# Turning the SwiGLU product f by 32x32 blocks on VectorE and a round trip through DRAM

## The chip, the cores and the metric

One core of a Trainium2 chip runs the whole kernel. The metric is device time in microseconds (us), and the median of several runs is compared. In the profile PE is TensorE (PEld its weight loads), DVE is VectorE, ACT is ScalarE, POOL is GpSimd and SP is SyncE, whose queue issues nearly all transfers.

## What is computed

A stack of transformer blocks on 256 tokens of width 1024, in fp32: four SwiGLU FFNs with a gMLP mixer and an MLA attention mixer between them, then a second block (retention and forgetting attention side by side) with a fifth FFN. The change touches the FFNs only:

```python
def swiglu(n, w_gate, w_up, w_down):
    return (jax.nn.silu(n @ w_gate) * (n @ w_up)) @ w_down

f = swiglu(rms_norm(h, ffn_pre_g[layer, 0]), ffn_w_gate[layer, 0], ffn_w_up[layer, 0], ffn_w_down[layer, 0])
h = h + 0.5 * rms_norm(f, ffn_post_g[layer, 0])
```

The inner width is 2816, so there are 11 groups of 256 inner columns.

## The kernel before

The 256 tokens are two tiles of 128 (called tile 0 and tile 1; `t` in the code). All weights stream once through the chip as chunks of 128 x 1024 values (512 KB) that both tiles use: tile 0 takes chunk s at step s, tile 1 five steps later (LAG). For each chunk SP loads `raw` (3 buffers, line 158), ACT rounds it to `hi` (line 337) and DVE computes the rest `lo` = raw - hi (line 338), both in rings of 9 buffers. Every fp32 product is then three fast matmuls, hi by hi, lo by hi and hi by lo (lines 167 to 169).

An FFN walks over the 11 groups. For group j, `up(j)` takes four chunks and gives `g`, 128 tokens by 256 gate and 256 up columns, in PSUM. ACT applies Tanh (`th`, line 364), DVE forms (th + 1) * gate (line 365) and f (line 367): 128 tokens by 256 inner columns. The product with w_down needs f with the inner columns on the partitions. `turn(j)` does that two steps later: two 128x128 transposes on PE into PSUM (`tr`, line 376), from where ACT and DVE make the pair `fth`, `ftl` (lines 337 and 338 again). `down(j-1)` takes two chunks of w_down and adds to the accumulators `a`, after `up(j)`. So in the middle of an FFN the work repeats with a period of one group for both tiles: six chunks, 72 matmuls, two Tanhs, six hi, six lo and two turns. Below this is called a round.

`later(st, n, fn)` puts a function off by n steps of its tile. The program is written in that order, but a scheduler at build time places each engine's instructions by priority, so the order on each engine comes from it. Each engine runs its own list strictly in order.

The two lines that decide when f is turned and used are

```python
later(st, 2, turn, j)
if 0 < j < NG - 2 * last:
    yield from down(j - 1)
```

Of the kernel before, what the change touches and what calls it, by code (L numbers as in the profile page):

```python
# [9 lines left out]
F32 = mybir.dt.float32  # L10
F32R = mybir.dt.float32r
# [5 lines left out]
P = 128  # L17
D = 1024
KD = D // P
FF = 2816  # L20
NG = FF // 256
# [88 lines left out]
def body(ctx: ExitStack, tc: tile.TileContext, a: dict, out: bass.AP, stop=None, dbg=None):  # L110
    nc = tc.nc
    V, S, G, PE = nc.vector, nc.scalar, nc.gpsimd, nc.tensor

    base = ctx.enter_context(tc.tile_pool(name="base", bufs=1))
    ring = ctx.enter_context(tc.tile_pool(name="ring", bufs=1))
    psg = ctx.enter_context(tc.tile_pool(name="psg", bufs=2, space=bass.MemoryType.PSUM))
    psa = ctx.enter_context(tc.tile_pool(name="psa", bufs=1, space=bass.MemoryType.PSUM))
    pst = ctx.enter_context(tc.tile_pool(name="pst", bufs=2, space=bass.MemoryType.PSUM))

    def f32(x):  # L120
        return x.bitcast(F32)
# [70 lines left out]
    def later(st, n, fn, *args):  # L192

        st.later.append([n + 1, fn, args])
# [128 lines left out]
    def acc_tile(st):  # L323
        return [psa.tile([P, 512], F32, name=f"a{st.t}{q}") for q in range(2)]

    def g_tile():
        return psg.tile([P, 512], F32, name="g")
# [8 lines left out]
    def split(hi, lo, src):  # L336
        S.copy(hi, src)  # L337
        V.tensor_tensor(lo, src, f32(hi), op=ALU.subtract)  # L338

    def rows_gemm(acc, lhs, w, k, first, last):  # L340

        for q in range(2):
            mm3(acc[q], sl(lhs, slice(None), k), sl(w, slice(None), slice(512 * q, 512 * q + 512)), first, last)

    def unit(st, ps, lhs=None, nq=4, nk=2, n=512):

        for q in range(nq):
            w = yield
            k_gemm(ps, lhs or st.xt, w, nk * q, q == 0, q == nq - 1, nk, n)
# [7 lines left out]
    def ffn(st, inner={}, last=False):  # L357
        fts = {}

        def up(j):  # L360
            ps = g_tile()
            yield from unit(st, ps)
            th = base.tile([P, 256], F32, name="th", tag="th", bufs=2)
            S.activation(th, ps[:, :256], AF.Tanh, scale=st.ch)  # L364
            V.scalar_tensor_tensor(th, th, 1.0, ps[:, :256], op0=ALU.add, op1=ALU.mult)  # L365
            f = base.tile([P, 256], F32, name="f", tag="f", bufs=2)
            V.scalar_tensor_tensor(f, th, st.cc, ps[:, 256:], op0=ALU.mult, op1=ALU.mult)  # L367
            fts[j] = f
            st.mark = f[:, 0:1]
            later(st, 2, turn, j)  # L370

        def turn(j):
            f = fts[j]
            tr = pst.tile([P, 4, P], F32, name="tr")
            for k in range(2):
                PE.transpose(tr[:, k, :], f[:, k * P:(k + 1) * P], ident)  # L376
            pool, n = (enter("last"), 6) if last and j > 5 else (base, 3)
            hi = pool.tile([P, 2, P], F32R, name="fth", tag="fth", bufs=n)
            lo = pool.tile([P, 2, P], F32R, name="ftl", tag="ftl", bufs=n)
            split(hi, lo, tr[:, :2, :])  # L380
            fts[j] = hi, lo

        def down(j):
            if j == 0:
                st.acc = acc_tile(st)
            for k in range(2):
                w = yield
                f = fts[j]
                rows_gemm(st.acc, f, w, k, j + k == 0, j == NG - 1 and k == 1)

        for j in range(NG):
            yield from up(j)
            if 0 < j < NG - 2 * last:
                yield from down(j - 1)
            if callable(inner.get(j)):
                inner[j]()
            elif j in inner:
                yield from inner[j]
        for j in range(NG - 1 - 2 * last, NG):
            yield from down(j)  # L400
# [614 lines left out]
    def enter(name):  # L1015
        if name not in pools:
            pools[name] = [tc.alloc_tile_pool(name=name, bufs=1), 0]
        return pools[name][0]
# [92 lines left out]
    n = len(chunks)  # L1111
# [38 lines left out]
def layout(i):  # L1150

    c = np.ascontiguousarray
    o = {}

    def cols(w, unit, nk=2):

        k, n = w.shape
        return c(w.reshape(k // (P * nk), nk, P, n // unit, unit).transpose(3, 0, 2, 1, 4)).reshape(-1, P, nk * unit)

    def rowsw(w):  # L1160

        return w.reshape(-1, P, w.shape[1])

    def gu(g, u):
        both = np.stack([g.reshape(D, NG, 256), u.reshape(D, NG, 256)], 2).reshape(D, NG * 512)
        return cols(both, 512)

    fl = [(i["ffn_w_gate"][l, k], i["ffn_w_up"][l, k], i["ffn_w_down"][l, k]) for l in range(2) for k in range(2)]
    fl.append((i["w_gate_2"][0], i["w_up_2"][0], i["w_down_2"][0]))
    for n, (g, u, d) in enumerate(fl):  # L1170
        o[f"gu{n}"] = gu(g, u)
        o[f"dn{n}"] = rowsw(d)
    o["win"] = cols(i["gmlp_w_in"][0], 512)
    o["wgo"] = rowsw(i["gmlp_w_out"][0])
    o["wdq"] = cols(i["mla_w_dq"][0], 512)
    o["wdkv"] = cols(i["w_dkv"], 320)
    uq = i["mla_w_uq"][0].reshape(512, NH, 192)
    o["wuqr"] = cols(c(uq[:, :, P:]).reshape(512, 512), 512)
    o["wuq"] = cols(c(uq[:, [0, 2, 4, 6, 1, 3, 5, 7], :P]).reshape(512, 1024), 512)
    ukv = i["w_ukv"].reshape(256, NH, 256)  # L1180
    o["wukv"] = np.concatenate([cols(c(ukv[:, :, k * P:(k + 1) * P]).reshape(256, 1024), 512) for k in range(2)])
    wo = i["mla_w_o"][0].reshape(NH, P, D)
    o["wo"] = c(wo[[0, 2, 4, 6, 1, 3, 5, 7]])
    w2 = i["w_in_2"][0]
    big = np.concatenate([w2[:, 1536:2048], w2[:, 2048:2560], w2[:, 2560:3072], w2[:, 0:512], w2[:, 512:1024],
                          w2[:, 1024:1536], w2[:, 3080:4104], w2[:, 4104:5128]], 1)
    o["w2"] = cols(big, 512)
    o["w2f"] = c(w2[:, 3072:3080].reshape(8, P, 8).transpose(1, 0, 2)).reshape(P, 64)
    o["wro"] = rowsw(i["w_ret_o_2"][0])
    o["wfo"] = rowsw(i["w_fox_o_2"][0])  # L1190
    o["wout"] = rowsw(i["w_out_2"][0])
    gl = [i["ffn_pre_g"][0, 0], i["ffn_pre_g"][0, 1], i["ffn_pre_g"][1, 0], i["ffn_pre_g"][1, 1], i["mix_pre_g"][0],
          i["mix_pre_g"][1], i["kv_norm_g"], i["kv_a_norm_g"], i["mla_q_norm_g"][0], i["g_mix_2"][0], i["g_ffn_2"][0], i["g_ret_norm_2"][0],
          np.concatenate([i["g_fox_q_2"][0]] * 2), np.concatenate([i["g_fox_k_2"][0]] * 2)]
    o["pre"] = np.stack([gl[k] for k in (4, 1, 2, 5, 3, 9)])
    o["kva"], o["qn"] = i["kv_a_norm_g"].reshape(1, 256), i["mla_q_norm_g"].reshape(1, 512)
    o["gains"] = c(np.concatenate([g.reshape(-1, P).T for g in gl], 1))
    o["ffn_post_g"] = c(i["ffn_post_g"].reshape(4, D))
    o["mix_post_g"] = c(i["mix_post_g"])
    o["gmlp_ln_g"] = c(i["gmlp_ln_g"])  # L1200
    o["gmlp_ln_b"] = c(i["gmlp_ln_b"])
    o["b_forget_2"] = c(i["b_forget_2"])
    o["ws"] = c(i["gmlp_w_s"][0].transpose(2, 0, 1)).reshape(P, 16 * P)
    o["bs"] = c(i["gmlp_b_s"][0].T)
    o["x"] = c(i["x"][0])
    o["positions"] = c(i["positions"].reshape(2, P).T)
    o["c1"], o["c2"] = constants()
    return o
# [49 lines left out]
```

## Time and profile before

| | us |
|---|---|
| median of three runs | 1397.67 (1396.39 to 1398.02) |
| the profiled execution | 1396.79 |
| its span (first to last instruction) | 1394.9 |
| PE busy | 1376.0, 99% |
| DVE busy | 957.0, 69% |
| ACT busy | 717.2, 51% |
| DMA, mean | 182 GB/s |

Busy time is the union of an engine's instructions; issuing a transfer or waiting is not counted as busy. Matmuls overlap in the rows, so the step from one start to the next tells what a matmul costs. A row's idle time is what passed on that engine just before the instruction, with what ended it.

### The profile page before, as it was taken

The page shows a single profiled execution, that of the slowest core. Times are in us where ns is not written, and L with a number is a line of the kernel's source. Part 1 is how long each engine was busy: PE and PEld are TensorE (multiplying, and loading weights), DVE is VectorE, ACT ScalarE, POOL GpSimd, SP SyncE. Part 2 cuts the span into 40 slices and gives each one's busy share as a digit, 9 for nine tenths or more (in the row PEclk, how much of TensorE's full clock was granted, in tenths as well). Part 3 has the DMA queues.
Part 4 walks back from the last instruction along what each step waited for, and adds up shares of the span by engine and source line. Part 5 has one row for each costly group of instructions (what it writes and reads, how often), then busy time and mean ns, then how long its engine had stood idle before and what let it go on. Part 6 is the DMA issues. An engine that isn't in the chain of part 4 may idle for free.

```text
span 1394.9 us, 17750 instructions
## 1 busy us (share of the span) xinstructions
PE 1376.0 (99%) x6402; PEld 1125.1 (81%) x6402; DVE 957.0 (69%) x1530; ACT 717.2 (51%) x1043; POOL 59.7 (4%) x81
## 2 busy tenths in 40 slices
PE   8999999999999999999999999999999999999998
PEld 5888887887788887888877888888878788888887
DVE  7775579977757558775569676665677865765554
ACT  6644456555544445544456655444567544544442
POOL 0000020000000001000001010000020000000000
PEclk9999999999999999999999999999999999999999
DMA  7666667554566664666655336666544355565662
GB/s 250 201 220 185 188 250 222 157 191 151 181 191 217 186 192 143 201 220 195 188 190 179 124 130 183 202 201 191 199 137 150 119 168 183 171 190 185 192 185 88
DMA packets 71656, 254.45 MB, mean 182 GB/s; under 512 B 8592, under 2 KB 10000, under 8 KB 71184
## 3 DMA queue, kind: packets, MB, share of 16 engines
q1 hardware_dynamic: 70992, 252.78, 57.7%
q8 instruction: 51, 0.84, 0.2%
q10 hardware_dynamic: 576, 0.52, 0.1%
q14 instruction: 37, 0.30, 0.1%
HBM read 252.23 MB, written 1.05 MB: 182 GB/s over the span
## 4 chain that ended last, share of the span: by engine, by line
PE 87%; DVE 6%; ACT 2%; DMA 2%; issue 1%; POOL 1%; SPq 0%; DVEq 0%; ACTq 0%; POOLq 0%
PE g L167 16%; PE g L168 16%; PE g L169 16%; PE a L169 11%; PE a L167 11%; PE a L168 11%; DVE lo L338 2%; PE tr L376 2%; PE tr L217 2%; DMA raw<-in_win 1%; POOL sm L145 1%; ACT hi L337 1%; DMA raw<-in_gu 1%; PE tr L459 0%; PE tr L722 0%
## 5 line engine op out<-in xcount | busy, mean ns | idle before, releaser
L338 DVE TENSOR_TENSOR lo<-raw,hi 128x1024 fp32r<-128x1024 f32 (+2 forms) x462 | 560.8, 1216 | 307.2 <-ACT hi L337 305.6
L337 ACT CAST hi<-raw 128x1024 fp32r<-128x1024 f32 (+2 forms) x462 | 481.2, 1044 | 428.8 <-PE g L169 205.7
L167 PE MATMUL g<-hi,xth 128*128 128x512 f32 x1040 | 414.3, 398 | 2.2 <-ACT hi L337 1.8
L168 PE MATMUL g<-lo,xth 128*128 128x512 f32 x1040 | 407.6, 392 | 2.0 <-DVE lo L338 2.0
L169 PE MATMUL g<-hi,xtl 128*128 128x512 f32 x1040 | 406.3, 391 | 0.0
L167 PEld LDWEIGHTS g<-hi,xth 128*128 128x128 f32 x1040 | 195.4, 188 | 43.0 <-ACT hi L337 3.5
L169 PEld LDWEIGHTS g<-hi,xtl 128*128 128x128 f32 x1040 | 195.4, 188 | 41.3 <-DVE sm L255 0.2
L168 PEld LDWEIGHTS g<-lo,xth 128*128 128x128 f32 x1040 | 195.6, 188 | 41.0 <-DVE lo L338 3.7
L167 PE MATMUL a<-hi,fth 128*128 128x512 f32 x440 | 175.7, 400 | 0.0
L168 PE MATMUL a<-lo,fth 128*128 128x512 f32 x440 | 172.0, 391 | 0.0
L169 PE MATMUL a<-hi,ftl 128*128 128x512 f32 x440 | 171.9, 391 | 0.0
L169 PEld LDWEIGHTS a<-hi,ftl 128*128 128x128 f32 x440 | 82.6, 188 | 17.4
L364 ACT ACTIVATE th<-g,ch 128x256 f32<-128x256 f32 x110 | 52.3, 475 | 86.4 <-PE g L169 85.2
L168 PEld LDWEIGHTS a<-lo,fth 128*128 128x128 f32 x440 | 82.8, 188 | 15.5
L167 PEld LDWEIGHTS a<-hi,fth 128*128 128x128 f32 x440 | 82.6, 188 | 15.5
L167 PE MATMUL a<-hi,xth 128*128 128x512 f32 x232 | 94.0, 406 | 0.7 <-ACT xth L337 0.6
L168 PE MATMUL a<-lo,xth 128*128 128x512 f32 x232 | 91.0, 394 | 0.0
L169 PE MATMUL a<-hi,xtl 128*128 128x512 f32 x232 | 90.9, 395 | 0.0
L365 DVE SCALAR_TENSOR_TENSOR th<-th,g 128x256 f32<-128x256 f32 x110 | 45.9, 418 | 43.5 <-ACT th L364 43.4
L337 ACT CAST fth<-tr 128x256 fp32r<-128x256 f32 x110 | 40.5, 369 | 37.6 <-PE tr L376 37.6
L367 DVE SCALAR_TENSOR_TENSOR f<-th,cc,g 128x256 f32<-128x256 f32 x110 | 52.8, 480 | 3.5
L167 PEld LDWEIGHTS a<-hi,xth 128*128 128x128 f32 x232 | 43.6, 188 | 10.3 <-ACT xth L337 2.1
(318 smaller groups left out, 1187.0 us busy)
## 6 DMA issues: line engine op xcount, KB each, us to landing
raw<-in_gu SPq DMA_DIRECT2D x220, 512.0 KB, 3.6
raw<-in_dn SPq DMA_DIRECT2D x110, 512.0 KB, 3.9
raw<-in_w SPq DMA_DIRECT2D x40, 512.0 KB, 3.3
raw<-in_win SPq DMA_DIRECT2D x32, 512.0 KB, 4.3
raw<-in_wgo SPq DMA_DIRECT2D x16, 512.0 KB, 3.6
raw<-in_wo SPq DMA_DIRECT2D x8, 512.0 KB, 3.3
raw<-in_wout SPq DMA_DIRECT2D x8, 512.0 KB, 3.3
gn<-in_pre SPq DMA_DIRECT2D x6, 512.0 KB, 5.3
```

The lines of the kernel that those rows point to most:

```text
L145: G.tensor_tensor(o, i, hp if up else hn[:, :n], op=ALU.pow)
L167: PE.matmul(o, l[0], r[0], start=start, stop=False)
L168: PE.matmul(o, l[0], r[1], start=False, stop=False)
L169: PE.matmul(o, l[1], r[0], start=False, stop=stop_)
L217: PE.transpose(tr[:, k, :], src[:, (4 * ngroup + k) * P:(4 * ngroup + k + 1) * P], ident)
L337: S.copy(hi, src)
L338: V.tensor_tensor(lo, src, f32(hi), op=ALU.subtract)
L364: S.activation(th, ps[:, :256], AF.Tanh, scale=st.ch)
L365: V.scalar_tensor_tensor(th, th, 1.0, ps[:, :256], op0=ALU.add, op1=ALU.mult)
L367: V.scalar_tensor_tensor(f, th, st.cc, ps[:, 256:], op0=ALU.mult, op1=ALU.mult)
L376: PE.transpose(tr[:, k, :], f[:, k * P:(k + 1) * P], ident)
```

## The change

For 10 of the 11 groups PE no longer turns f. DVE turns it in place by 32x32 blocks (`V.transpose`, into `ft`), which leaves the blocks themselves where they were: partition block a holds columns i of its own 32 tokens. `away` writes `ft` to a DRAM tile `far` (128 pieces of 1 KB), and `back` reads it again with four transfers, one for each block c of 32 columns, so that the blocks a of the tokens come to lie side by side on the 32 partitions (32 x 4 pieces of 256 bytes each). `parts` makes `fth` and `ftl` from the SBUF tile `fr`. All five transfers are issued from ACT's queue. The last group of each FFN keeps `turn`. `ft` shares its buffers with `th`, `fr` with `f`. The columns come out in another order within a group, so the rows of w_down are laid out in that order on the host, before the launch.

```diff
+    dram = ctx.enter_context(tc.tile_pool(name="dram", bufs=1, space=bass.MemoryType.DRAM))
@@ up(j)
             st.mark = f[:, 0:1]
-            later(st, 2, turn, j)
+            if j == NG - 1:
+                later(st, 2, turn, j)
+                return
+
+            ft = base.tile([P, 256], F32, name="ft", tag="th", bufs=2)
+            V.transpose(ft, f)
+            later(st, 1, away, j, ft)
+
+        def away(j, ft):
+            far = dram.tile([4, 32, 4, 64], F32, name="far", bufs=4)
+            nc.scalar.dma_start(far.rearrange("a i c r -> (a i) (c r)"), ft)
+            later(st, 0, back, j, far)
+
+        def back(j, far):
+            fr = base.tile([P, 4, 64], F32, name="fr", tag="f", bufs=2)
+            for c in range(4):
+                nc.scalar.dma_start(fr[32 * c:32 * c + 32], far[:, :, c, :].rearrange("a i r -> i a r"))
+            later(st, 0, parts, j, fr.rearrange("p a (k i) -> p k a i", k=2))
+
+        def parts(j, fr):
+            f = fts[j] = f_tiles(j)
+            split(*(x.rearrange("p k (a i) -> p k a i", a=4) for x in f), fr)
@@ layout
-        o[f"dn{n}"] = rowsw(d)
+        d = d.reshape(NG, 4, 2, 32, D)
+        o[f"dn{n}"] = np.concatenate([d[:-1].transpose(0, 2, 1, 3, 4).reshape(-1, P, D), d[-1].reshape(2, P, D)])
```

`f_tiles(j)` only names the pool and makes the two result tiles, as `turn` did before.

ACT's list in one round in the middle of the first FFN, before (`th_1327` is tile 1's Tanh, `th_1344` tile 0's; `hi` are weight chunks; numbers name single buffers):

```order
L337 CAST hi_1293<-raw_1291 128x1024
L337 CAST hi_1311<-raw_1309 128x1024
L337 CAST hi_1334<-raw_1332 128x1024
L364 ACTIVATE th_1327<-g_1239,ch_290 128x256
L337 CAST hi_1357<-raw_1355 128x1024
L364 ACTIVATE th_1344<-g_1259,ch_168 128x256
L337 CAST hi_1383<-raw_1381 128x1024
L337 CAST hi_1409<-raw_1407 128x1024
L337 CAST fth_1377<-tr_1374 128x256
L337 CAST fth_1397<-tr_1394 128x256
```

The same round after the change, from tile 0's Tanh to the end of its turn (lines are those of the changed file, one higher here; `far_1305` and `fr_1328` belong to tile 1, `far_1319` and `fr_1346` to tile 0):

```order
L365 ACTIVATE th_1292<-g_1199,ch_170 128x256
L381 DMA far_1305<-ft_1278 128x256
L338 CAST hi_1335<-raw_1333 128x1024
L338 CAST hi_1363<-raw_1361 128x1024
L387 DMA fr_1328<-far_1305 32x4x64
L381 DMA far_1319<-ft_1297 128x256
L387 DMA fr_1328<-far_1305 32x4x64 x3
L387 DMA fr_1346<-far_1319 32x4x64 x4
L338 CAST fth_1357<-fr_1328 128x256
L338 CAST hi_1385<-raw_1383 128x1024
L338 CAST hi_1403<-raw_1401 128x1024
L338 CAST fth_1373<-fr_1346 128x256
```

Before, the two casts of the turned f stood behind each other and read PSUM; now ten transfers stand in the list, and the first read of tile 0 stands three issues behind the write it reads from.

PE's list at the end of tile 1's part of a round, before (`tr` are the turns, `a00` and `a01` tile 0's accumulators):

```order
L376 MATMUL tr_1374<-cst_70,f_1330 128x128 x2
L167 MATMUL a00_331<-hi_1334,fth_1263 128x512
L168 MATMUL a00_331<-lo_1335,fth_1263 128x512
L169 MATMUL a00_331<-hi_1334,ftl_1264 128x512
L167 MATMUL a01_332<-hi_1334,fth_1263 128x512
L168 MATMUL a01_332<-lo_1335,fth_1263 128x512
L169 MATMUL a01_332<-hi_1334,ftl_1264 128x512
L376 MATMUL tr_1394<-cst_70,f_1347 128x128 x2
L167 MATMUL g_1373<-hi_1223,xth1_225 128x512
```

And after, from the end of tile 1's `up` on (`g_1181` is tile 1's, `g_1199` tile 0's, `a10` and `a11` are tile 1's accumulators):

```order
L170 MATMUL g_1181<-hi_1093,xtl1_230 128x512
L168 MATMUL a10_477<-hi_1111,fth_1211 128x512
L169 MATMUL a10_477<-lo_1112,fth_1211 128x512
L170 MATMUL a10_477<-hi_1111,ftl_1212 128x512
L168 MATMUL a11_478<-hi_1111,fth_1211 128x512
L169 MATMUL a11_478<-lo_1112,fth_1211 128x512
L168 MATMUL g_1199<-hi_1239,xth0_130 128x512
L170 MATMUL a11_478<-hi_1111,ftl_1212 128x512
L168 MATMUL a10_477<-hi_1136,fth_1211 128x512
L169 MATMUL a10_477<-lo_1137,fth_1211 128x512
L170 MATMUL a10_477<-hi_1136,ftl_1212 128x512
```

The turns are gone from the list, and the two tiles' matmuls now lie in another order: tile 0's last `up` chunk stands between the parts of tile 1's `down`.

## Rows read from the trace of the kernel before

**Rows 1.** The page: span, busy time of each engine, and the chain's shares by engine.
```profile
span 1394.9 us, 17750 instructions
...
PE 1376.0 (99%) x6402; PEld 1125.1 (81%) x6402; DVE 957.0 (69%) x1530; ACT 717.2 (51%) x1043; POOL 59.7 (4%) x81
...
PE 87%; DVE 6%; ACT 2%; DMA 2%; issue 1%; POOL 1%; SPq 0%; DVEq 0%; ACTq 0%; POOLq 0%
...
```

**Rows 2.** The chain that ended last, in shares by engine and line.
```profile
...
by line: PE g L167 16.1%; PE g L168 16.0%; PE g L169 16.0%; PE a L169 10.8%; PE a L167 10.8%; PE a L168 10.7%; DVE lo L338 1.8%; PE tr L376 1.7%; PE tr L217 1.7%; issue 1.5%; DMA raw<-in_win 1.0%; POOL sm L145 1.0%; ACT hi L337 1.0%; DMA ra
...
```

**Rows 3.** Busy time by stretch; this one is mid first FFN, columns in its head.
```profile
...
core 0: us, PE busy (x) PEld busy (x) DVE busy (x) ACT busy (x) POOL busy (x), PEclk, DMA share, GB/s
26.00:178.00 152.00, 152.00 (x687) 124.93 (x686) 98.62 (x162) 76.76 (x104) 2.04 (x3) 1.00 0.65 201
...
```

**Rows 4.** Timeline of PE: start and length in us; 27 matmuls from the first row to the second.
```profile
...
109.62 0.39 PE L167 MATMUL g<-hi,xth 128*128 128x512 f32 x1
...
115.51 0.40 PE L169 MATMUL a<-hi,ftl 128*128 128x512 f32 x1
115.75 0.38 PE L376 MATMUL tr<-cst,f 128*128 128x128 f32 x2
115.88 0.48 PE L167 MATMUL a<-hi,fth 128*128 128x512 f32 x1
116.20 0.40 PE L168 MATMUL a<-lo,fth 128*128 128x512 f32 x1
...
```

**Rows 5.** Timeline of ACT, same stretch; in brackets the idle time before and what ended it.
```profile
...
110.50 0.47 ACT L364 ACTIVATE th<-g,ch 128x256 f32<-128x256 f32 x1 [1.67 <-PE g L169]
110.87 1.04 ACT L337 CAST hi<-raw 128x1024 fp32r<-128x1024 f32 x1
111.86 0.48 ACT L364 ACTIVATE th<-g,ch 128x256 f32<-128x256 f32 x1
113.26 1.05 ACT L337 CAST hi<-raw 128x1024 fp32r<-128x1024 f32 x1 [0.93 <-PE a L169]
...
127.36 0.47 ACT L364 ACTIVATE th<-g,ch 128x256 f32<-128x256 f32 x1 [1.67 <-PE g L169]
...
```

**Rows 6.** Groups by line and shape: count, busy us, mean ns, idle us before.
```profile
...
L338 DVE TENSOR_TENSOR lo<-raw,hi 128x1024 fp32r<-128x1024 f32 x454 | 554.9, 1224 | 303.0 <-ACT hi L337 301.4
L337 ACT CAST hi<-raw 128x1024 fp32r<-128x1024 f32 x454 | 476.0, 1050 | 424.6 <-PE g L169 204.7 <-PE a L169 155.3 <-DMA raw<-in_gu 28.8
...
L367 DVE SCALAR_TENSOR_TENSOR f<-th,cc,g 128x256 f32<-128x256 f32 x110 | 52.8, 480 | 3.5
L364 ACT ACTIVATE th<-g,ch 128x256 f32<-128x256 f32 x110 | 52.3, 475 | 86.4 <-PE g L169 85.2 <-DVE cc L259 1.1
L365 DVE SCALAR_TENSOR_TENSOR th<-th,g 128x256 f32<-128x256 f32 x110 | 45.9, 418 | 43.5 <-ACT th L364 43.4
...
L338 DVE TENSOR_TENSOR ftl<-tr,fth 128x256 fp32r<-128x256 f32 x110 | 42.4, 417 | 5.9 <-ACT fth L337 5.8
...
L337 ACT CAST fth<-tr 128x256 fp32r<-128x256 f32 x110 | 40.5, 369 | 37.6 <-PE tr L376 37.6
...
L337 ACT CAST xth<-y 128x256 fp32r<-128x256 f32 x16 | 6.3, 402 | 7.0 <-DVE y L228 6.8
...
```

**Rows 7.** DMA queues, and issues by tile: count, KB each, median us to landing.
```profile
...
q1 hardware_dynamic: 70992, 252.78, 57.7%
...
q10 hardware_dynamic: 576, 0.52, 0.1%
...
out<-h SPq DMA_DIRECT2D x4, 128.0 KB, 1.9
out<-h ACTq DMA_DIRECT2D x4, 128.0 KB, 2.9
...
gain<-in_gains SPq DMA_DIRECT2D x1, 42.0 KB, 2.8
wfr<-in_w2f SPq DMA_DIRECT2D x1, 32.0 KB, 3.9
...
```

**Rows 8.** Line 1098, the stores of the result: issue in ns, and us to landing.
```profile
...
L1098 ACTq DMA_DIRECT2D out<-h x4: 338/338/374, 1383.5 to 1392.0; - x4
...
DMA to landing us min/median/max: 1.7/1.9/4.0
```

**Rows 9.** Line 158, the weight loads: us to landing.
```profile
...
DMA to landing us min/median/max: 3.0/3.6/9.8
```

**Rows 10.** The same line in the first FFN alone, 26 to 178 us.
```profile
...
DMA to landing us min/median/max: 3.3/4.1/6.7
```

More of the change, by code (lines that the diff above doesn't have):

```diff
@@ L369, in up, with f_tiles @@
             st.mark = f[:, 0:1]
-            later(st, 2, turn, j)
+            if j == NG - 1:
[13 more added lines that the diff above has]
+            later(st, 0, parts, j, fr.rearrange("p a (k i) -> p k a i", k=2))
+        def f_tiles(j):
+            pool, n = (enter("last"), 6) if last and j > 5 else (base, 3)
+            return tuple(pool.tile([P, 2, P], F32R, name=x, tag=x, bufs=n) for x in ("fth", "ftl"))
+        def parts(j, fr):
+            f = fts[j] = f_tiles(j)
+            split(*(x.rearrange("p k (a i) -> p k a i", a=4) for x in f), fr)
         def turn(j):
@@ L376, in turn @@
                 PE.transpose(tr[:, k, :], f[:, k * P:(k + 1) * P], ident)
[L377 to L381, printed above, removed]
+            fts[j] = f_tiles(j)
+            split(*fts[j], tr[:, :2, :])
         def down(j):
```

## The prediction, made before the changed kernel was run

> **What bounds the kernel now.** I read the page first. TensorE (PE) is busy for 1376.0 of 1394.9 us, ScalarE (ACT) for 51% and VectorE (DVE) for 69% [rows 1]; the chain that ended last lies on PE for 87% and on DVE, ACT and DMA together for 10% [rows 1]. A busy PE says little by itself, since matmuls overlap, so I went to stretches: in the first FFN PE has work in every one of 152 us, at the full granted clock of 2.4 GHz [rows 3]. In the timeline of PE 26 steps from the matmul at 109.62 to that at 115.51 take 5.89 us, so one 128x512 matmul costs 0.2265 us of PE, whatever its row calls its length [rows 4]. A pair of turns (the two 128x128 transposes of f) stands in that rhythm as a hole: from 115.51 to 116.20 there are 0.69 us where two steps would take 0.453, so the pair costs 0.236 us [rows 4]. Now ACT: between the Tanh of one round of groups and that of the next lie 16.86 us (110.50 to 127.36) [rows 5]. A round is one group of both token tiles, that is six chunks, 72 matmuls and two pairs: 72 x 0.2265 = 16.31, and 0.55 is left for two pairs. ACT waits for PE there, not the reverse: of 424.6 us of idle time before the hi casts, 360.0 end with a matmul [rows 6]. So PE sets the pace of the FFNs, and what leaves its queue there leaves the span, as long as nobody else becomes the slower one.
>
> **What the change removes.** 100 pairs of turns (10 groups, 2 tiles, 5 FFNs). At 0.236 us that is 23.6 us. From below: the chain gives the turns' line 1.7% of 1394.9 us, 23.7 us for 110 pairs, 0.216 each, so 21.6 for 100 [rows 2]. From above: the 0.55 us of a round, 0.27 a pair, 27 [rows 5]. I take 23.6, since it was read at the pair itself.
>
> **What it adds on DVE.** One 32x32 block turn of 128x256 for each group and tile. No such row exists; other 128x256 operations take 0.418 and 0.480 us, and one on four times the elements 1.224 [rows 6], so 0.42 to 1.22, and I take 0.48, that of the f product which reads and writes the same tile shape. 100 x 0.48 is 48 us on an engine that is idle for 31% [rows 1]: nothing on the path. Its one reader is the write: tile 0's turn stands behind a lo and is done some 7.0 us after tile 1's Tanh (3.4 for the 15 matmuls between the two Tanhs, then 0.47, 0.34, 1.05, 1.22 and 0.48), and the round worked out below wants it at 7.7; at 1.22 us it would come just then. The cast and the difference that make fth and ftl stay in number, but read SBUF instead of PSUM; a cast of the same size from SBUF takes 0.402 against 0.369 [rows 6], 3 us on ACT in all, hidden.
>
> **What it adds on ACT and the DMA queues.** Five issues for each group and tile, 500 in all; one on ACT's queue takes 0.338 us [rows 8], 169 us on an engine with 678 us free. The packets: 128 written and 512 read, and 16 completions for each of five, 720 a turn, 72,000 in all. ACT's queue now has 576 packets for 0.1% [rows 7]; by that these cost 12.5% (6 to 19% with the rounding), and the engines' share goes from 57.7% to about 70%. They don't fill up, but loads, writes and reads will land somewhat later than today.
>
> **The new waits.** In the order of the changed kernel ACT does, in a round: Tanh of tile 1, two hi, Tanh of tile 0, write of tile 1, two hi, first read of tile 1, write of tile 0, three more reads, four reads of tile 0, fth of tile 1, two hi, fth of tile 0. ACT works in order, so the first read of tile 0 holds it until the write three issues earlier has landed, and fth holds it until the reads have. Behind these waits stand the two hi casts, then the next Tanh and two more hi; PE waits for the hi, and DVE's lo and SyncE's next weight load follow each hi. What can set the pace is therefore this round on ACT, DVE and SP: Tanh 0.47, hi 1.05, its lo 1.22, the weight load whose buffer this lo freed, hi 1.05, one read's issue 0.34, the write's landing, 1.01 for three more issues, the reads' landing, fth 0.37. The fixed parts are 5.51 us [rows 6, 8]; three landings come on top, and the whole must stay under PE's 16.31, so the three may sum to 10.8 us. The loads land after 3.6 us in the median of the kernel, 3.0 at best [rows 9], and after 4.1 in the first FFN [rows 10]; I take 3.9. For the write: stores of 128 KB land after 1.7 to 4.0, with 1.9 the median, 2.9 from ACT's queue [rows 7, 8]; I take 2.6, near the median of all, and above it, because loads are in flight here. For reads in 256-byte pieces the nearest rows are 2.8 (128 pieces of 336 bytes) and 3.9 (128 of 256 bytes), both on the queue of the weight loads [rows 7]; the 1.7 of a store is the lower end, 3.9 the upper [rows 7, 8]. I take 3.0. Sum 9.5, round 15.0 us: 1.3 us of cover. With the worst rows, 4.1 + 4.0 + 3.9 = 12.0, it is 17.5 us, 1.2 over PE's pace. If the cover is gone, every us of landing costs 50 us in the kernel (50 rounds). The Trainium skill (DMA: Bandwidth & Descriptors, Specifications) says that pieces under 512 bytes miss the line rate because they are read, modified and written; by that one would take 3.9 for the reads and have a round of 15.9 us. The row of 336-byte pieces at 2.8 doesn't show such a loss.
>
> **Is f there in time?** From the last matmul of g to the first use of fth there are 73 matmuls in most rounds of the changed order, 62 or more where an FFN starts, 52 for the very first group: 16.5, 14.0 and 11.8 us. The way takes Tanh 0.47, 0.42 and 0.48 on DVE, turn 0.48, issue 0.34, write 2.6, four issues 1.35, read 3.0, fth and ftl 0.79, so 9.9 us, plus what stands ahead in the queues (one lo of 1.22 on DVE before tile 0's turn, a hi or two). Enough in the rounds, thin at the starts of FFNs. Ten starts (5 FFNs, 2 tiles) at 0 to 1 us: I add 2 us, not in a row but from this lack of spare.
>
> **Sum.** The profiled execution took 1396.8 us; minus 23.6 plus 2 gives 1375.2. The median of the three runs lies 0.9 above the profiled one, so **1376 us**. The weights' new row order is laid out before the launch and costs the chip nothing.
>
> **Rivals.** (1) *The forecast*, PE keeps the pace: 1369 to 1386. For it: 1.3 us of cover in the round, and 2.9 us more between the lo of a chunk (Tanh, hi, lo: 2.74 us) and its use 25 matmuls (5.7 us) after the same event. (2) *ACT's round takes a part*: landings sum to 10.8 to 11.3, the round is 16.3 to 16.9, the gain shrinks to nothing bit by bit: about 1390. Today's round of 16.86 is the point where the gain is gone. (3) *ACT's round becomes the bound and the kernel slower*: from landings of 11.35 us together on. Its price with the worst rows (12.0): round 17.51, 0.65 us over today's, 50 rounds, 32 us, so 1430; with loads slowed further to 4.5 by the new packets 52 us, 1450. For it: writes of 4.0 do stand in the trace, and a load is nearly always in flight; against: all three must be bad at once, round after round. The Trainium skill (VectorE: DVE Perf Modes, The three transpose paths and Rules for kernel authors) sends a 128x128 turn to TensorE, because VectorE turns 32x32 blocks alone, and calls a turn by a plain DMA with strides 19 times slower than the turning DMA; by that rule this rival would be the outcome. No row here has a DMA that moves single elements, and this one keeps runs of 64 elements. (4) *The turn was not the loss*: PE loses as much at starts of FFNs, waiting for fth, as it gains, ten starts by 2.3 us: 1394 to 1400. Against: the changed order leaves 14 us there.
>
> **Chances.** (1) 0.67, (2) 0.08, (3) 0.16, (4) 0.09. Within 0.2%, about what a measurement of this kernel can tell from no change, is 1394.9 to 1400.5. Faster: 0.67 and most of (2), 0.73; same: the rest of (2) and most of (4), 0.10; slower: (3) and what (4) exceeds, 0.17. The range must leave out no more than 0.2: from 1368 (27 us saved and nothing lost) to 1400, which takes in (1), (2) and (4) and leaves out (3).
>
> **What would show it.** Right: rounds of about 16.3 us between Tanhs of one tile in mid-FFN, PE steps of 0.2265 without holes, ACT's wait before the first read of tile 0 at 1 to 2 us (2.6 less the three issues between) and ACT still idle for about 1 us before the next Tanh. Wrong: PE waiting for hi or lo in every round (3), or for fth where an FFN starts (4); writes or reads that land after 4 us or more; block turns of more than 1.2 us.

## The result, and the profile after

The changed kernel takes 1497.3 us (median of 4 runs, 1495.1 to 1503.0) against 1397.2 for the kernel before: 1.072 times as long, interval 1.069 to 1.075. The forecast was 1376. The profiled execution took 1495.1 us, its span is 1493.3. Line numbers of the changed kernel are one higher up to line 369 (hi and lo 338 and 339, matmuls 168 to 170, Tanh 365); the block turn is line 376, the write 381, the reads 387.

The page, as [rows 1, 7] show it of before: busy times, queues, the chain's shares by engine, and the issues with KB and median us to landing.

```profile
span 1493.3 us, 18105 instructions
...
PE 1394.7 (93%) x6202; PEld 1108.7 (74%) x6202; DVE 984.4 (66%) x1630; ACT 702.0 (47%) x1041; POOL 57.8 (4%) x81
...
q10 hardware_dynamic: 72576, 26.77, 6.7%
...
PE 18%; DMA 13%; DVE 6%; issue 3%; ACT 3%; ACTq 1%; POOL 1%; DVEq 0%; SPq 0%; POOLq 0%
...
raw<-in_gu SPq DMA_DIRECT2D x220, 512.0 KB, 4.2
raw<-in_dn SPq DMA_DIRECT2D x110, 512.0 KB, 5.0
...
far<-ft ACTq DMA_DIRECT2D x100, 128.0 KB, 4.2
fr<-far ACTq DMA_DIRECT2D x400, 32.0 KB, 3.7
```

PE has 200 matmuls fewer. The chain can be followed back here only to 807.8 us, so that its shares of the span add up to less than half: PE has 274 of the chain's 683 us, 40%, where it had 87% [rows 1]. What PE and ACT wait for is in the tables of waits (us in all, times, longest), first PE's longest:

```profile
PE a L168 <- ACT fth L338: 62.5, 42, 4.6
```

```profile
ACT fth L338 <- DMA fr<-far: 297.7, 53, 10.3
ACT hi L338 <- DMA raw<-in_gu: 155.2, 118, 5.3
ACT hi L338 <- PE a L170: 61.0, 48, 3.9
ACT hi L338 <- PE g L170: 35.2, 27, 3.0
```

The roles are swapped. ACT's hi casts waited for PE before [rows 6]; now they wait mostly for loads, ACT waits 298 us at fth, and PE waits for fth. The stretches of the first FFN that answer to [rows 3] show what such a wait does (columns as there):

```profile
26.00:190.00 164.00, 150.60 (x628) 118.84 (x627) 100.76 (x173) 69.70 (x98) 0.30 (x2) 0.97 0.64 202
100.00:104.00 4.00, 0.00 (x0) 0.00 (x0) 0.60 (x2) 0.00 (x0) 0.00 (x0) 0.99 0.37 110
104.00:110.00 6.00, 5.37 (x13) 4.22 (x14) 4.87 (x7) 3.91 (x6) 0.00 (x0) 0.50 0.37 112
110.00:112.00 2.00, 2.00 (x9) 1.59 (x8) 0.94 (x3) 1.43 (x3) 0.00 (x0) 0.81 0.99 334
112.00:118.00 6.00, 6.00 (x28) 4.97 (x27) 4.37 (x6) 2.09 (x2) 0.00 (x0) 1.00 0.72 232
```

PE stands still from 100 to 104.6; when it starts again its granted clock is 0.50, that is 1.2 GHz, for 6 us, and the DMA engines are busy for 0.37 of the time, against 0.64 over the stretch: SP issued no load from 97.1 to 106.8. Over the span the mean granted clock is 0.989 (1.000 before). That is 16 us of PE's time (0.011 x 1493); no run shows that the span is longer by it, since PE is not in the loop shown below.

One round on ACT, to be held against [rows 5] (ACTq rows are issues of transfers; seven in a row are one line):

```profile
106.68 0.46 ACT L365 ACTIVATE th<-g,ch 128x256 f32<-128x256 f32 x1
...
111.21 0.34 ACTq L381 DMA_DIRECT2D far<-ft  x1
...
114.56 0.31 ACTq L387 DMA_DIRECT2D fr<-far  x1
115.21 0.34 ACTq L381 DMA_DIRECT2D far<-ft  x1
115.58 7.03 ACTq L387 DMA_DIRECT2D fr<-far  x7
122.72 0.41 ACT L338 CAST fth<-fr 128x256 fp32r<-128x256 f32 x1 [7.47 <-DMA fr<-far]
...
125.24 0.47 ACT L365 ACTIVATE th<-g,ch 128x256 f32<-128x256 f32 x1
```

And SP's loads in the same time and just before:

```profile
93.48 3.62 SPq L159 DMA_DIRECT2D raw<-in_dn  x2
106.81 6.38 SPq L159 DMA_DIRECT2D raw<-in_gu  x4
114.84 2.03 SPq L159 DMA_DIRECT2D raw<-in_dn  x2
125.37 0.33 SPq L159 DMA_DIRECT2D raw<-in_gu  x1
```

From Tanh to Tanh it is 18.56 us, 16.86 before. Seven reads that would take some 3 us to issue take 7: after the three that belong to tile 1 ACT waits for tile 0's write. No weight load goes out from 116.9 to 125.4.

The chain, cut to a stretch of the fourth FFN, shows the loop that sets the pace there (start, us, what; "issue" is time with no wait, here much of it DVE at work):

```profile
990.50 0.45 DVE ft L376
...
990.98 5.39 DMA far<-ft
...
998.43 0.40 ACT fth L338
998.83 0.96 ACT hi L338
...
1002.20 4.68 DMA raw<-in_gu
...
1006.90 1.06 ACT hi L338
...
1009.12 0.45 DVE ft L376
...
1009.60 4.21 DMA far<-ft
...
1014.76 1.76 DMA fr<-far
1016.51 0.40 ACT fth L338
...
1019.15 3.60 DMA raw<-in_gu
...
1027.45 4.90 DMA far<-ft
```

Write, the reads' issues, fth, hi, lo, the load into the buffer that this lo freed, hi, lo, and then the block turn of tile 0, which stands behind that lo on DVE, and the next write. PE is not in it. The first turn of the loop is 18.62 us (990.98 to 1009.60), 10.07 of it landings (5.39 + 4.68) and 8.55 fixed.

The second turn is 17.85 us. Its row of 1.76 us is not the landing of one read. The fth at 1016.51 is tile 1's, as in ACT's list, and the reads that it needs went out before tile 0's write had landed. Here are the last two of them, line 387 from 1011.6 to 1012.1:

```profile
L387 ACTq DMA_DIRECT2D fr<-far x2: 455/455/455, 1011.2 to 1011.7; - x2
...
DMA to landing us min/median/max: 4.8/4.9/5.1
```

The last one landed at 1016.45, 0.8 us after ACT had issued tile 0's last read. So 0.9 of the 1.76 us are issues and 0.8 are a wait, and the second turn has 8.6 us of landings (4.21 + 0.83 + 3.60) and 9.2 fixed.

The same was counted, from issues and landings, in the 30 rounds in which tile 1 turns one of its groups 3 to 8. Tile 0's write lands after 5.1 us in the median (3.4 to 6.3), and the four issues behind it take 1.9. By then tile 1's reads have landed in 20 of the 30 rounds; in the other 10 fth waits for them for 0.1 to 0.8 us more. From fth to the next write of tile 0 it is 11.2 us in the median.

The sum: from the first Tanh to the last the five FFNs take 972.6 us, 894.7 before (ACT's timeline), so 77.9 of the 98.4 us of span lie there, 1.56 for each of 50 rounds. Of the other 20, 19.3 lie in the tails of the FFNs, from the last Tanh to the last product with w_down (88.6 us in all for 69.3 before, PE's timeline; in the first FFN alone 24.5 for 14.1). A small part of that is work that moved: 17 matmuls of `down`, 3.9 us, stood before the last Tanh and stand behind it now.

### The profile page after: what moved, and what is told of

It is laid out like the page before. It is cut to its first block, busy times and chain, and to the rows that moved or that the text cites. A ratio compares the mean times of both kernels' runs of the same rounds, so it can differ in the third digit from the quotient of the medians.

```text
span 1493.3 us, 18105 instructions
## 1 busy us (share of the span) xinstructions
PE 1394.7 (93%) x6202; PEld 1108.7 (74%) x6202; DVE 984.4 (66%) x1630; ACT 702.0 (47%) x1041; POOL 57.8 (4%) x81
## 5 line engine op out<-in xcount | busy, mean ns | idle before, releaser
L168 PE MATMUL a<-hi,fth 128*128 128x512 f32 x440 | 181.0, 414 | 65.2 <-ACT fth L338 62.5
L339 DVE TENSOR_TENSOR ftl<-fr,fth 128x256 fp32r<-128x256 f32 x100 | 42.1, 421 | 237.7 <-ACT fth L338 208.3
L338 ACT CAST fth<-fr 128x256 fp32r<-128x256 f32 x100 | 40.3, 403 | 297.7 <-DMA fr<-far 297.7
L170 PE MATMUL a<-hi,ftl 128*128 128x512 f32 x440 | 175.1, 405 | 4.6 <-DVE ftl L339 4.1
L169 PE MATMUL a<-lo,fth 128*128 128x512 f32 x440 | 176.5, 402 | 0.6 <-DVE lo L339 0.6
L366 DVE SCALAR_TENSOR_TENSOR th<-th,g 128x256 f32<-128x256 f32 x110 | 45.4, 413 | 11.4 <-ACT th L365 11.2
```

Source lines behind the costliest of these rows:

```text
L168: PE.matmul(o, l[0], r[0], start=start, stop=False)
L169: PE.matmul(o, l[0], r[1], start=False, stop=False)
L170: PE.matmul(o, l[1], r[0], start=False, stop=stop_)
```

## Experiments: which part of the trip costs

**Three kernels that take the trip apart.** Without the trip:

```diff
-            later(st, 1, away, j, ft)
+            later(st, 1, parts, j, ft.rearrange("p (a k i) -> p k a i", a=4, k=2))
```

> The trip through DRAM is left out: fth and ftl are made from ft, the block-turned tile itself (so the block grid is not moved and the output is another), with the two casts, the block turn on DVE and the removal of PE's turns kept. Theory (what costs is the trip, by ACT's waits for its landings): the whole saving of PE appears, 1397.2 - 23.6 = 1373.6, so 1370 to 1378. Rival (the block turn on DVE, or the order that the scheduler makes without the turns, is the loss): 1450 or more; a part of it would show as 1385 or more.

Measured: 1373.8 us (1372.4 to 1374.5), 23.8 less than before, tile 0's rounds from the seventh on 16.3 us (the last of the fifth FFN 14.8). The price of PE's turns and the cost at nothing of the block turn were right. Now the trip with reads that find their data landed long ago:

```diff
-            far = dram.tile([4, 32, 4, 64], F32, name="far", bufs=4)
+            far = dram.tile([4, 32, 4, 64], F32, name="far", bufs=6)
...
-            later(st, 0, back, j, far)
+            was, st.far = getattr(st, "far", None) or far, far
+            later(st, 0, back, j, was)
```

> All five transfers stay on ACT's queue, but the reads of group j fetch what group j-1 wrote (so the data are the wrong group's), landed long ago: the wait for the write is gone from ACT, the wait of fth for its reads stays. Theory: the stall of 3.7 us a round before tile 0's first read goes (the share of reads in the wait stays), and the round drops from 18.4 us to under 17: 1385 to 1425. Rival (traffic): 1470 or more. Rival (the waits for the reads do it, not that for the write): 1450 to 1490.

Measured: 1407.7. And the trip with nobody who uses it:

```diff
+            st.ft = ft
...
-            later(st, 0, parts, j, fr.rearrange("p a (k i) -> p k a i", k=2))
+            later(st, 0, parts, j, st.ft.rearrange("p (a k i) -> p k a i", a=4, k=2))
```

> Write and reads go on as in the changed kernel, from ACT, but fth and ftl are made from ft, and nobody uses what the reads bring (the block grid is not moved, the output is another). Left of the waits is ACT's for the write before the first read, and the buffers. Theory: most of the loss is that wait on ACT, so 1420 to 1480. Rival (fth's wait for the reads is the loss): 1374 to 1395. Rival (traffic): 1470 or more, with loads that land as late as now.

Measured: 1464.9. If the parts add up, the four times give three prices: the wait for the write 1497.3 - 1407.7 = 90 us, the wait of fth for the reads 1497.3 - 1464.9 = 32, and all else of the trip (issues, traffic) 1407.7 - 1373.8 - 32 = 1.5. That they add up is an assumption (the scheduler gives each kernel its own order, and no kernel here tests it), and the 1.5 is no price of traffic by itself, since traffic also lengthens the waits. But traffic alone as the cause falls without the assumption: the kernel with all the packets and issues and without the wait for the write is 90 us faster. The wait for the write is three quarters. In the kernel without use it was PE's wait for hi that showed it:

```profile
PE g L168 <- ACT hi L338: 32.2, 26, 3.7
```

**Shorter loads.** The landings were suspected to be long because loads fly with them (the edit in part):

```diff
-        nc.sync.dma_start(raw[:, :n], src)
+        h = n if i < 3 else n // 2
+        nc.sync.dma_start(raw[:, :h], src[:, :h])
```

> The changed kernel with weight loads of half the bytes (256 KB instead of 512 KB); hi and lo of both halves are made from the half that was loaded. Left out: half of the weights. Theory (the write and the reads land late because weight loads are in flight with them): the write's median landing falls from 4.2 to under 3.2 us, the reads' from 3.7 to under 3, the three landings sum to less than 10.8 and PE sets the pace again: 1374 to 1400. Rival (the landings are long by their own small pieces and their number): write and reads land as now, and only the load's share goes: 1430 to 1480.

Measured: 1389.6 (two runs, 1389.3 and 1389.9), with these landings on its page:

```profile
raw<-in_gu SPq DMA_DIRECT2D x217, 256.0 KB, 2.7
raw<-in_dn SPq DMA_DIRECT2D x110, 256.0 KB, 3.1
far<-ft ACTq DMA_DIRECT2D x100, 128.0 KB, 2.9
fr<-far ACTq DMA_DIRECT2D x400, 32.0 KB, 2.7
```

Write and reads are what they were, in pieces and number, and land 1.3 and 1.0 us sooner. In the 30 rounds counted above tile 0's write now takes 3.1 us in the median. With 8.6 to 9.2 fixed and 2.7 to 3.1 for the load the loop would be 14.4 to 15.4 us, under PE's 16.31, and most late rounds are 16.0 to 16.6 again. (The kernel before was not run with half the loads.) The trace of the changed kernel says the same: of its writes the 9 that meet at most one load between issue and landing take 1.8 us in the median, the 69 that meet three 4.2, the 17 that meet four 4.8 (counted from the issues and landings of both). So it is the loads in flight that make the landings long, and the loop that makes them cost.

**Another queue.** All five transfers from POOL's queue:

```diff
-            nc.scalar.dma_start(far.rearrange("a i c r -> (a i) (c r)"), ft)
+            nc.gpsimd.dma_start(far.rearrange("a i c r -> (a i) (c r)"), ft)
```

> The write and the four reads issue from POOL's queue instead of ACT's; the same bytes and pieces move. Theory (ACT works in order and is held by landings that collide with weight loads; PE then waits for fth, and the loads wait behind the hi casts that ACT did not do): ACT waits for nothing but the reads at fth, for which the order leaves 79 matmuls, 17.9 us, in mid-FFN, so 1375 to 1405. Rival (the traffic itself: 72,000 more packets slow the loads, whoever issues them): 1470 or more. Second rival (issuing from POOL is slow by itself, and fth comes late): 1405 to 1470 with idle ACT before fth.

Measured: 1502.8 (1500.9 to 1506.3). A miss: ACT is free of the wait for the write, but still waits 254 us for the reads at fth, and nothing is gained. POOL's timeline shows why:

```profile
110.81 0.56 POOL L381 DMA_DIRECT2D far<-ft  x1 [7.04 <-DVE th L366]
115.11 0.55 POOL L387 DMA_DIRECT2D fr<-far  x1 [3.74 <-issue]
115.66 0.56 POOL L381 DMA_DIRECT2D far<-ft  x1
116.21 1.63 POOL L387 DMA_DIRECT2D fr<-far  x3
120.58 2.17 POOL L387 DMA_DIRECT2D fr<-far  x4 [2.74 <-DMA far<-ft]
```

Tile 0's ft is ready at 112.8 and its write goes out at 115.66: it stands behind tile 1's first read, which waits for tile 1's write. Then only the reads from POOL:

```diff
-                nc.scalar.dma_start(fr[32 * c:32 * c + 32], far[:, :, c, :].rearrange("a i r -> i a r"))
+                nc.gpsimd.dma_start(fr[32 * c:32 * c + 32], far[:, :, c, :].rearrange("a i r -> i a r"))
```

> The write issues from ACT, the four reads from POOL's queue. In the kernel with all five on POOL tile 0's write stood for 2.9 us behind tile 1's first read, which waited for tile 1's write. Theory (it is the place in an in-order queue that costs): tile 0's write goes out at once, ACT waits for no write, 1400 to 1470. Rival (turn, write, reads and fth are too long a chain for 79 matmuls, whatever the queue): 1480 or more, with PE waiting for fth as now.

Measured: 1433.7 (1431.0 and 1436.3). 69 of that kernel's 105 us are gone with the writes alone on another queue, where they pass the waiting reads. What is left is PE's wait for fth (24.0 us, 16 times) and the first three rounds of each FFN (32 us in all over the kernel before, by tile 0's Tanhs).

**Using f a group later.** `down(j - 2)` in place of `down(j - 1)`, with the reads four steps later and held back by a POOL copy, and fth one step after them (the edit in part):

```diff
-            if 0 < j < NG - 2 * last:
-                yield from down(j - 1)
+            if 1 < j < NG - last:
+                yield from down(j - 2)
...
@@ back
+            G.tensor_copy(fr[:, 0, 0:1], sts[1].mark)
```

> The same turn, the same five transfers from ACT, but a group later: down(j-2) instead of down(j-1) follows up(j), a POOL copy of a column of tile 1's next f gates the reads, and fth is made two steps after them, so the order leaves some 146 matmuls (33 us) from g to the use of fth and every landing has at least 10 us. Theory (the transfers cost by being waited for at once in ACT's list): nearly all of PE's saving appears, rounds of 16.3 us, 1374 to 1390. Rival (traffic: the loads land later by it and PE starves): 1400 or more. Rival (the wait only moves to fth): rounds over 17 us and PE waiting for fth, 1420 or more.

> A control for the kernel with the later use: the kernel before, PE's turns kept, with down(j-2) instead of down(j-1). Theory: the order of the products is worth little by itself, since PE has work all the time in mid-FFN: 1392 to 1402. Rival (a gain or a loss of that kernel comes from the order, not from the turns): over 6 us off 1397.2.

Measured: 1426.3 (1421.4 to 1429.8), and the control with PE's turns 1411.2. Both theories failed: the order costs 14 by itself, and the trip 15 on top of it. From the first to the last Tanh the FFNs take 862.7 us against the control's 885.5. That looks like 22.8 of the 23.6 us, but less work is done in that stretch. Here is the first FFN of both, first this kernel, then the control, with only those instructions that have to do with fth (stretch and its length, then PE's busy time and count):

```profile
17.20:188.30 171.10, 46.54 (x141) 26.11 (x141) 8.40 (x20) 8.03 (x20) 1.00 0.75 225
17.00:191.50 174.50, 46.00 (x150) 28.01 (x150) 8.81 (x21) 7.76 (x21) 1.00 0.66 200
```

With ftl's products and in all five FFNs 77 matmuls of `down`, 17 us, have moved behind the last Tanh. From the first Tanh to the last product with w_down the FFNs take 983.1 us, 10 more than the control's 972.9, though 100 turns are gone. So the rounds gained little, and the next expectation, which takes the 23 us as gained, starts from a false reading. A second version ended the FFNs in the old order:

```diff
+def downs(j, last):
+    if j < 2 or last and j > 8:
+        return []
+    if j == 9 - last:
+        return [j - 2, j - 1]
+    return [9] if j == 10 else [j - 2]
```

> As the kernel with the later use, but the ends of the FFNs are as in the kernel before: groups 0 to 8 make the trip (90 turns), 9 and 10 are turned on PE, and down(7) and down(8) both follow up(9), so that down(9) and down(10) stand where they stood. Theory (the rounds gained their 23 us there, and the loss lay in the longer ends of the FFNs): 90 x 0.236 = 21.2 us less than the control of the same order, and 1376 to 1390 if that order costs nothing. Rival (the traffic or the reads' waits eat the gain in the rounds themselves): 1397 or more, with FFNs as long from the first Tanh to the last as the control's.

> The control: the kernel before, PE's turns kept, with the order of the products of the kernel above (down two groups late from group 2 to 8, then caught up). Theory: the 14 us of the first control lay at the ends of the FFNs, which are now as before: 1394 to 1402. Rival (using f two groups late costs by itself): 1405 or more.

Measured: 1420.1 and 1408.2. Both theories failed: the order costs 11 also so, and the trip costs 12 on top of it. From the first Tanh to the last the FFNs take 907.0 us against the control's 909.2, with as many products of f in between (1196 and 1198), so nearly all of the 21.2 us is lost in the rounds themselves, as the rival had it. What loses it was not found: no single wait of PE stands out (fth 9.1 us, 8 times). In both kernels with the later use the loads of w_gate and w_up land after 4.3 us in the median, in both controls after 3.6, so a part of the traffic in this loss is not excluded.

**One tile alone**, here tile 0 (`st.t == 0` for tile 1; the edit in part, without the two operations on DVE):

```diff
+            plain = j == NG - 1 or st.t == 1
...
-            if j == NG - 1:
+            if plain:
```

> Only tile 0 makes the trip (50 of 100); tile 1 keeps PE's turns. So that both tiles use the same rows of w_down, tile 0's f is written in the trip's column order by two operations on DVE instead of one. In ACT's list the write and the four reads now stand apart by two or three casts, and fth stands two hi behind the reads; there is no second write in the way. Theory (the loss is the wait of a read three issues behind its write, and of fth right behind its reads; what work stands between covers it): 11.8 us saved, little lost, 1384 to 1400. Rival (each trip costs its share of the loss, wherever it stands): half of 100, 1440 to 1450.

> Only tile 1 makes the trip (50 of 100), tile 0 keeps PE's turns; otherwise as the run above. Here only one hi stands between the write and the first read in ACT's list (1.05 us, and what the hi waits for). Theory (uncovered wait decides): more of the write's 4 us shows than with tile 0, so 1390 to 1420 and not under tile 0's time. Rival (each trip costs its share): 1440 to 1450, both tiles alike.

Measured: tile 0 alone 1432.8 (1431.6 to 1433.2), tile 1 alone 1415.6 (1413.9 to 1423.9). My expectation for tile 0 failed, and the order of the two is the other way round. Tile 0's timeline on ACT:

```profile
124.17 0.34 ACTq L388 DMA_DIRECT2D far<-ft  x1
124.55 0.37 ACT L338 CAST fth<-tr 128x256 fp32r<-128x256 f32 x1 [2.23 <-PE g L170]
124.82 1.05 ACT L338 CAST hi<-raw 128x1024 fp32r<-128x1024 f32 x1
128.65 2.01 ACTq L394 DMA_DIRECT2D fr<-far  x4
130.75 1.99 ACT L338 CAST hi<-raw 128x1024 fp32r<-128x1024 f32 x2 [4.88 <-issue]
```

ACT's casts behind the write are done at 125.87; it stands 2.8 us until the write has landed, with the hi casts and the next loads behind it. This kernel's chain is led by the write and the loads again (9.6% and 8.6% of the span), and most rounds are 17 to 18 us. With tile 1 alone nearly all are 16.6 us from the seventh on, 16.86 less one pair of turns, and from 110 to 146 us the chain lies on PE alone: there the wait falls where ACT had nothing that PE needed soon. What that kernel loses lies in the first three rounds of the FFNs (21 us in all, by tile 0's Tanhs). So the casts between the two transfers did not decide. That what stands behind the second one does is read from these timelines; no run tests it.

**The middle of the FFNs alone.** Tile 1 in groups 5 to 9 only; both tiles there, with tile 0's reads from POOL; the same with all reads from POOL. The edits of the first and of the second, each in part; the third has `nc.gpsimd` for both tiles:

```diff
+            plain = j == NG - 1 or st.t == 0 or j < 5
...
-            if j == NG - 1:
+            if plain:
```

```diff
-            if j == NG - 1:
+            if j == NG - 1 or j < 5:
...
-                nc.scalar.dma_start(fr[32 * c:32 * c + 32], far[:, :, c, :].rearrange("a i r -> i a r"))
+                (nc.scalar if st.t else nc.gpsimd).dma_start(fr[32 * c:32 * c + 32], far[:, :, c, :].rearrange("a i r -> i a r"))
```

> Only tile 1 makes the trip, and only in groups 5 to 9 (25 of 100 turns); the others are PE's, as in the kernel before. With tile 1's trip in all ten groups the late rounds took 16.6 us, 0.25 under the kernel before, and the first five of an FFN took 2 to 10 us more in all. Theory (where the wait for the write and the reads lies beside work that ACT waits for anyway, nothing but PE's saving is left; what was lost was lost at the starts): 25 x 0.236 = 5.9 us less, 1389 to 1394. Rival (the trip's traffic costs something in every round, seen only in the sum): 1396 or more.

> Both tiles make the trip in groups 5 to 9 (50 turns); the writes and tile 1's reads issue from ACT, tile 0's reads from POOL's queue, so that no queue has a second trip's wait behind the first. Theory (a wait of its own in a queue of its own costs nothing as long as fth is in time): 50 x 0.236 = 11.8 us less, 1384 to 1394. Rival (write and reads under two loads take 4 us each whatever the queue, and tile 0's way is too long): rounds over 16.85 in groups 6 to 9, 1400 to 1420.

> As the run above, but the reads of both tiles issue from POOL, in groups 5 to 9 alone; the writes stay on ACT. With this split in all ten groups the late rounds took 16.3 to 16.9 us. Theory (starts of the FFNs hold the loss of that kernel): 1388 to 1400. Rival (the waits for fth spread over all rounds): 1405 or more, half of that kernel's 36 us.

Measured: 1403.9 (1400.2 to 1407.7), 1401.9 (1400.1 to 1412.1) and 1395.8 (1393.9 to 1398.1). The first two missed their expectations; the third is no different from the kernel before (0.9994, interval 0.9985 to 1.0003). In the first the rounds with a trip take 16.6 us as forecast, but the first of them 18.4 to 19.2, where 16.8 stood. In the third the last four rounds of an FFN are 16.2 to 16.9 but for three, and PE once waits 7.3 us for x of the norm at an FFN's end. So group 9 was left to PE as well, with all reads on POOL, and then groups 4 to 8 were tried (the edit of the first, in part):

```diff
-            if j == NG - 1:
+            if not 5 <= j <= 8:
```

> As the kernel with both tiles' reads on POOL in groups 5 to 9, which tied with the kernel before; group 9 is now PE's turn too, so that 40 turns are left and no landing is waited for at the end of an FFN, where a wait of 7.3 us for x of the norm stood once. Theory (what is left of the loss lies at the ends of the FFNs): 40 x 0.236 = 9.4 us less, 1386 to 1393. Rival (the loss lies in every round with a trip): 1394 to 1400.

> The same with groups 4 to 8, 50 turns. Theory: 11.8 us less, 1384 to 1391, unless the round of group 4, in which the loads for the norm's weights also move, loses what it gains. Rival (the loss lies in every round with a trip): 1394 to 1402.

Measured: 1391.0 (1387.5 to 1391.8) against 1397.9, ratio 0.9945 [0.9932, 0.9957], and 1394.0 (1392.3 to 1394.6), 0.9969 [0.9957, 0.9980]. Groups 5 to 8 with the reads on POOL are as forecast: 6.9 us (0.55%) less than the kernel before, of the 9.4 that 40 turns are worth. The ends were part of the loss. With group 4 the forecast failed: it gives back more than it brings, by what is not shown.

## Why the prediction was wrong, point by point

- **The saving: right.** 23.6 us forecast, 23.8 measured without the trip.
- **The block turn: right.** 0.44 us (433 to 448 ns) for 0.48 taken; beside the path. The casts from SBUF take 0.403 for 0.402.
- **Packets and issues: right in number, too dear in share.** 72,000 new packets, as counted, at 6.6% of the engines' time for 12.5 taken; what they and the issues cost beside the waits is 1.5 us, if the parts above add up. An issue took 0.34 us for a write and 0.45 in the median for a read, for 0.338.
- **The landings: wrong one by one, right in sum by luck.** Tile 0's write, the one in the loop, took 5.1 us in the median of the rounds for 2.6 (4.2 over all writes). The load took 4.68 and 3.60 in the two turns shown for 3.9. The reads' 3.0 us are not in the loop as a term behind the write: fth needs tile 1's reads, which fly beside tile 0's write (5.0 us in the median of the last one) and are waited for at most 0.8 us. Forecast 9.5 in a row; the two turns have 10.1 and 8.6. The landings are dear because they collide with loads; that the loads bunch because ACT stands is read from SP's rows and not tested.
- **The round: the step that failed.** The prediction drew a loop of 5.51 us fixed parts from Tanh to Tanh; the two turns of the chain have 8.6 and 9.2. Tanh isn't in it. In it are, in the first turn, the four reads' issues with the gaps between them (996.37 to 998.43, 2.06 us, for 1.35), the lo, ftl and issue between hi and the next load (2.41, for one lo of 1.22), and, left out altogether, the last lo and tile 0's block turn on DVE (1.64, from the end of hi at 1007.96). The prediction knew that this turn stands behind a lo and put it 7.0 us after tile 1's Tanh, wanted at 7.7; it is done 8.6 us after it (982.38 to 990.95), since the hi ahead of that lo waits for a load. Counted as work beside the round, it was a part of it, and closed the loop from one write to the next.
- **The sum of the round, term by term** (means of the rounds counted above). From fth to the next write, with a load in it, the prediction's own terms give 8.4 us; the chip took 11.4. The write was 2.6 and took 4.9. Issues and reads behind it were 4.0 and took 2.2. So 15.0 became 18.5: 3.0 more for the part between fth and the write, 2.3 more for the write, 1.8 less for the reads. By its own sum each of the first two, put right alone, would have given a round over PE's 16.31 (18.0 and 17.3).
- **The cover of 1.3 us** was no cover: most rounds in mid-FFN take 17.8 to 19.5 us, and the 50 rounds are 77.9 us longer in all.
- **The rivals.** (3) came true, ACT's round as the bound, at 100 us for its 32 to 52, with chance 0.16. Its price was short, since the loop is longer than drawn and the tails of the FFNs add 19. It was to show as PE waiting for hi or lo each round; PE waits for fth, 62.5 us in 42 waits: in ACT's list fth stands ahead of the hi. Of (4), PE waiting for fth where an FFN starts, there is a little: 10.6 of these 62.5 us fall into the first three rounds.
- **Small pieces, and whose work a turn is.** The row of 336-byte pieces spoke against a loss by small pieces, and the runs agree: with half the loads the same 256-byte pieces land in 2.7 us. The rule of the Trainium skill (DMA: Bandwidth & Descriptors, Specifications) on pieces under 512 bytes isn't what the time shows. The rule of the Trainium skill to leave a 128x128 turn to TensorE (VectorE: DVE Perf Modes, Rules for kernel authors) named the outcome; the run without the trip, 23.8 us faster than the kernel before, shows that it isn't DVE's turn that loses, but the way of the blocks.

What stays open: why the tails of the FFNs grow by 19 us, most in the first one, and by what the later use of f, with its long cover, still lost 12 us and more.

## What to carry to other kernels

When a change adds a wait to an in-order engine, draw the whole loop from one such wait to the next, through every engine that it passes, and count as fixed what stands in front of the waiting transfer too; a step that is "done in time" on another engine is part of the loop if what delays it hangs on the wait. Ask of each cast which transfer it waits for, and whether that one went out before or behind the wait. Price each landing with the loads in flight that the loop itself sends out next to it. If a round trip must be made, give writes and reads different queues, so that no write stands behind a read that waits, and leave out the ends of the stage, where nothing covers it.

## What the runs showed of the hardware

- The same 128 KB write lands after 1.8 us in the median where it meets at most one weight load and after 4.2 and 4.8 where it meets three and four; halving the loads brought its median from 4.2 to 2.9. The mean share of the DMA engines in the first FFN, 0.64, doesn't show this: it was 0.37 from 100 to 110 us and 0.99 in the two after that.
- After PE stood for 4.6 us its granted clock was 0.50 (1.2 GHz) until 110 and 1.00 again from 112 on. Shorter waits did not do this each time: from 112 to 200 us it stayed at 1.00, with four waits for fth of 1.1 to 1.7 us.
- One read of 32 KB was 144 packets on ACT's queue (57,600 of q10 for 400) and 32 on POOL's (12,800 for 400), at 4.0 us to land from POOL and 3.7 from ACT (medians of two kernels): fewer packets did not land sooner. An issue takes POOL 0.55 us, ACT 0.34 to 0.45.
